# Attention weights in two sets of buffers, up to three attention tiles under way, their value chain one turn later

## The chip, the cores and the metric

The program runs on one core of a Trainium2 chip. The metric is device time in microseconds; lower is better. TensorE (PE) does matmuls and transposes, VectorE (DVE), ScalarE (ACT) and GpSimd (POOL) do the element work, and SyncE (SP) issues the DMAs. Every engine works through its own queue in order.

## The reference, cut to what matters

One layer of a hybrid encoder runs over 2048 prompt frames and 32 sample frames (model width 1024, float32). A projection gives queries (8 heads of 64), keys and values (2 heads) and the input of a state-space scan. The attention is banded by chunks of 64 frames, with a learned sink per head:

```python
s = einsum('bnqgrd,bnkgd->bngrqk', q, k) * HEAD_DIM ** -0.5
m = maximum(max(s, axis=-1), sink)
p = exp(s - m[..., None])
p = p / (sum(p, axis=-1) + exp(sink - m))[..., None]
o = einsum('bngrqk,bnkgd->bnqgrd', p, v)
```

Each chunk sees its own 64 frames and the 128 before. Attention and scan outputs are normalised, joined and projected (`w_out`), and a gated feed-forward follows.

## The kernel before, in words

Float32 products are made of three matmuls on operands split into a high and a low part: `split` copies the high part on ScalarE and subtracts on VectorE, and `mm3` issues the three matmuls. The kernel has four stages. Stage A (to about 355 us) projects. Stage B (about 355 to 560 us) runs the 32 scan groups (tiles `v`, `y`, `w`), six deferred projections (`qp`, `kp`) and the first six attention tiles. Stage C (about 560 to 950 us) runs the other eleven attention tiles beside the scan's gate (`c_prep`, bank `cb`), the norms (`c_norm`) and the output projection (`c_out`, banks `co`). The feed-forward fills the rest.

Stages B and C interleave Python generators. `Flow(make, n, width, lag)` holds at most `width` of them, starts the next when the youngest has had `lag` turns, and gives each one turn per `step`, oldest first. A turn is what stands between two `yield`s. This gives the source order. The builder's planner then orders each engine's instructions: among those that are ready by its own estimate of time, the one earliest in source order goes first. The order is fixed when the kernel is built; on the chip an engine waits at the head of its queue.

An attention tile is 128 query frames, and its work for the two 64-frame halves is numbered o = 0 and 1. Its turns before the change: (1) load `qkv`; (2) split and transpose queries and keys (`qb`, `kb`); (3) and (4) scores (`s`) and `softmax` of half 0 and half 1 into `pbuf` 0 and 1; (5) `p_split` of half 0, first key head: transposes of the weights into `pt`, then the split into `th`, `tl`; (6) the second key head; (7) `p_values` of half 0 (`ob`) and `p_split` of half 1; (8) its second key head; (9) `p_values` of half 1; (10) the end. With width 2 and lag 5 a new tile starts every five turns at the soonest. `softmax` takes the maximum on VectorE, four exponentials and one for the sink on ScalarE, a sum and a reciprocal on VectorE, and one scaling of `pbuf` on GpSimd.

In stage C each pass of the loop gives one turn to attention, one to `c_prep`, one to `c_norm` and two (`CST`) to `c_out`, which takes about five passes per tile. An attention tile starts only when it is less than `NATT` = 6 ahead of the tiles that `c_out` has finished. `c_norm` squares the attention output (`sqa`, GpSimd), sums it (`sa`, VectorE), adds over partitions with two pairs of tiny matmuls (`rb`) and takes the power (`rso`, GpSimd); `c_out` fills two banks `co` per half of the width, and `t<-co,rso` on ScalarE and then VectorE empty them, which needs `rso`. Scores, `pt`, `ob`, `qb` and `kb` share two PSUM banks in stage B and rotate over these and the `cb` banks in stage C. `th` and `tl` have two buffers each. When all attention tiles are done, `ffn_open` opens the feed-forward's buffers.

Of the kernel before, what the change touches and what calls it, by code (L numbers as in the profile page):

```python
# [10 lines left out]
F32 = mybir.dt.float32  # L11
# [12 lines left out]
NT = NPT + 1  # L24
# [49 lines left out]
def hybrid_kernel(  # L74
# [10 lines left out]
    V, A, P, PE, SP = nc.vector, nc.scalar, nc.gpsimd, nc.tensor, nc.sync  # L85
# [17 lines left out]
    def f(a):  # L103
        return a.bitcast(F32)

    def cp(e, out, a):
        if e is A:
            act(out, a)
        else:
            e.tensor_copy(out, a)  # L110

    def split(hi, lo, src, eh, el):
        cp(eh, hi, src)
        tt(el, lo, src, f(hi), SUB)

    def mm(out, lhsT, rhs, start, stop, more=False):
        PE.matmul(out, lhsT, rhs, start=start, stop=stop, skip_group_check=more)  # L117
# [798 lines left out]
    pb_ = bin_.enter_context(tc.tile_pool(name="pb", bufs=1, reuse_waits="tile", side="right"))  # L916
# [92 lines left out]
    def bbank(shape, dt=F32, nm="ab"):  # L1009
        turn[0] += 1  # L1010
        if CBANK and turn[0] % 3:
            return CBANK[0](shape, dt, nm)
        if AS3 and not CBANK and turn[0] % 2:
            return AS3[0].tile(shape, dt, tag="ab", name=nm)
        return as2.tile(shape, dt, tag="ab", name=nm)
# [7 lines left out]
    ts(V, nsink, nsink, -1.0)  # L1023
    ts(V, nsinks, nsinks, -1.0)

    pe_ = [pb_.tile([128, 4, 256], F32, name=f"pbuf{o}") for o in range(2)]
    P.memset(pe_[0][:, :, 192:256], 0.0)
    P.memset(pe_[1][:, :, 0:64], 0.0)

    def kv_split(kf, vf, dst, n):  # L1030

        ks = pb2.tile([128, 2, 2, 2, HD], F32R, tag="ks", name="ks", bufs=1)
        hi = ks[0:n, :, 0]
        act(hi, kf.unsqueeze(2).to_broadcast([n, 2, 2, HD]))
        tt(V, ks[0:n, :, 1], kf.unsqueeze(2).to_broadcast([n, 2, 2, HD]), f(hi), SUB)
        kb = bbank([128, 4, 128], F32R, nm="kb")
        for i in range(4):
            PE.transpose(kb[:, i, 0:n], ks[0:n, i // 2, i % 2].rearrange("t a d -> t (a d)"), identr[0:n, 0:n])
        cp(A, dst, f(kb[:, :, 0:n]))
        vs = pb2.tile([128, 2, 2, 2, HD], F32R, tag="vs", name="vs", bufs=4)  # L1040
        hi = vs[0:n, :, 0]
        act(hi, vf.unsqueeze(2).to_broadcast([n, 2, 2, HD]))
        tt(P, vs[0:n, :, 1], vf.unsqueeze(2).to_broadcast([n, 2, 2, HD]), f(hi), SUB)
        return vs
# [18 lines left out]
    def p_split(pbuf, kbs, npair, kv):  # L1063

        nc_ = npair * 128
        pt = bbank([128, 2, 256], nm="pt")
        for i in range(npair):
            for kb in kbs:
                PE.transpose(pt[:, kb, i * 128:(i + 1) * 128], pbuf[:, kv * npair + i, kb * 128:kb * 128 + 128], ident)
        th = pb2.tile([128, 2, 256], F32R, tag="th", name="th")  # L1070
        tl = pb2.tile([128, 2, 256], F32R, tag="tl", name="tl")
        k0, k1 = kbs[0], kbs[-1] + 1
        split(th[:, k0:k1, 0:nc_], tl[:, k0:k1, 0:nc_], pt[:, k0:k1, 0:nc_], A, V)
        return th, tl

    def p_values(parts, vlist, kbs, npair, out):

        w = npair * 128
        ob = bbank([128, 2 * w], nm="ob")
        n = 3 * len(kbs)  # L1080
        for kv in range(2):
            th, tl = parts[kv]
            c = 0
            for kb in kbs:
                vs, kn = vlist[kb]
                vh, vl = (vs[0:kn, kv, i].rearrange("t a d -> t (a d)") for i in range(2))
                for a, b in ((vh, th), (vl, th), (vh, tl)):
                    mm(ob[:, kv * w:kv * w + w], a, b[0:kn, kb, 0:w], c == 0, c == n - 1)
                    c += 1
        obv = ob.rearrange("p (m x q) -> p m x q", m=4, x=2)  # L1090
        for x in range(2):
            cp(V if x else A, out[64 * x:64 * x + 64], obv[64 * x:64 * x + 64, :, x])
# [2 lines left out]
    atts = {}  # L1095

    def attention_tile(j):
        j = TILES[j]
        n = 128 if j < NPT else DEC
        qkv = pb2.tile([128, QKV], F32, tag="qkv", name="qkv", bufs=1)  # L1100
        SP.dma_start(qkv[0:n], qkv_d[j * 128:j * 128 + n])
        yield 1
        qs = pb2.tile([128, NH, 128], F32R, tag="qs", name="qs", bufs=1)
        qv = qkv[0:n, 0:512].rearrange("p (h d) -> p h d", d=HD)
        split(qs[0:n, :, 0:64], qs[0:n, :, 64:128], qv, A, P)
        qt = pb2.tile([128, NH * 128], F32R, tag="qt", name="qt", bufs=1)
        qw = n // 2 if j < NPT else n
        qtv = qt[:, 0:NH * n].rearrange("p (o h q) -> p h o q", h=NH, q=qw)
        for hb in range(2):
            qb = bbank([128, 4, 128], F32R, nm="qb")  # L1110
            for i in range(4):
                PE.transpose(qb[:, i, 0:n], qs[0:n, hb * 4 + i], identr[0:n, 0:n])
            cp(V if hb else A, qtv[:, hb * 4:hb * 4 + 4], f(qb[:, :, 0:n]).rearrange("p h (o q) -> p h o q", q=qw))
        kf = qkv[0:n, 512:640].rearrange("p (h d) -> p h d", d=HD)
        vf = qkv[0:n, 640:768].rearrange("p (h d) -> p h d", d=HD)
        kt = pb2.tile([128, 4, 256], F32R, tag="kt", name="kt")
        att = pat.tile([128, 4, 128], F32, tag="att", name="att", bufs=NATT)
        atts[j] = att
        if j < NPT:
            vcur = kv_split(kf, vf, kt[:, :, 128:256], n)  # L1120
            if j == TILES[0]:
                pkv = pb2.tile([128, 2, 128], F32, tag="ckv", name="pkv", bufs=1)
                SP.dma_start(pkv, qkv_d[(j - 1) * 128:j * 128, 512:768].rearrange("t (a d) -> t a d", a=2))
                vprev[0] = kv_split(pkv[:, 0].rearrange("p (h d) -> p h d", d=HD),
                                    pkv[:, 1].rearrange("p (h d) -> p h d", d=HD), kt[:, :, 0:128], 128)
            elif j:
                V.tensor_copy(kt[:, :, 0:128], f(vprev[1][:, :, 128:256]))
            vpt = [vprev[0], vcur]
            vprev[0], vprev[1] = vcur, kt
            yield 1  # L1130
            vlist = [(vpt[0], 128), (vcur, 128)]
            kbs = (0, 1) if j else (1,)
            for o in range(2):
                lo, hi = (64 * o, 192 + 64 * o) if j else (128, 192 + 64 * o)
                sp = [bbank([128, 2, 256], nm="s") for _ in range(2)]
                for pr in range(4):
                    for x in range(2):
                        mm(sp[pr // 2][:, pr % 2, lo:hi], qt[:, 512 * o + 128 * pr:512 * o + 128 * pr + 128],
                           kt[:, (pr // 2) * 2 + x, lo:hi], x == 0, x == 1)
                softmax(sp, pe_[o], lo, hi, nsink)  # L1140
                yield 1
            for o in range(2):
                parts = []
                for kv in range(2):
                    parts.append(p_split(pe_[o], kbs, 2, kv))
                    yield 1
                p_values(parts, vlist, kbs, 2, att[:, :, 64 * o:64 * o + 64])
        else:
            ckv = pb2.tile([128, 2, 128], F32, tag="ckv", name="ckv", bufs=1)
            SP.dma_start(ckv[:, 0], cache_k[0, 0].rearrange("t h d -> t (h d)"))  # L1150
            SP.dma_start(ckv[:, 1], cache_v[0, 0].rearrange("t h d -> t (h d)"))
            vc = kv_split(ckv[:, 0].rearrange("p (h d) -> p h d", d=HD), ckv[:, 1].rearrange("p (h d) -> p h d", d=HD),
                          kt[:, :, 0:128], 128)
            vo = kv_split(kf, vf, kt[:, :, 128:160], n)
            sp = bbank([128, 2, 256], nm="s")
            for kv in range(2):
                for x in range(2):
                    mm(sp[:, kv, 0:160], qt[:, 128 * kv:128 * kv + 128], kt[:, kv * 2 + x, 0:160], x == 0, x == 1)
            P.memset(pe_[0][:, 0:2, 160:192], 0.0)
            softmax([sp], pe_[0], 0, 160, nsinks)  # L1160
            yield 1
            parts = [p_split(pe_[0], (0, 1), 1, kv) for kv in range(2)]
            yield 1
            p_values(parts, [(vc, 128), (vo, DEC)], (0, 1), 1, att[:, :, 0:DEC])
        yield 1
# [23 lines left out]
    def stage(nm):  # L1189
        return pw1.tile([128, 512], F32, tag="tc", name=nm, bufs=TC)  # L1190

    fa = Flow(attention_tile, NT, 2, 5)
    n = 0
    while fd.next < fd.n or fd.live:
        for fl, st, lim in ((fm, FM, G), (fd, FDS, G), (fa, FAS, NATT)):
# [705 lines left out]
```

## Time and profile before

| | |
|---|---|
| median of 3 runs | 2361.86 us (2360.06 to 2366.63) |
| the profiled execution | 2357.34 us, of which its span is 2355.6 us |
| busy share of the span | PE 94%, PE weight load 87%, DVE 76%, POOL 56%, ACT 53% |
| granted TensorE clock, mean | 0.967 of full speed |

The busy share of PE is an average over stages. The change touches only the attention tiles, so the stretch to read is the one in which these run, from about 355 to 880 us. A granted clock of 1.0 is 2.4 GHz and 0.5 is 1.2 GHz; a value between is a mix of the two over the stretch. In lines of the trace L89 is the helper for two-operand element work, L101 that for ScalarE, L117 that for matmuls; L1069 is the transpose in `p_split`, L1354 the sum in `c_norm`.

### The profile page before, as it was taken

The numbers are of one execution on the slowest core, as the hardware profiler recorded it, in microseconds if no ns is written. First come the engines' busy times: TensorE is split into PE (matmuls) and PEld (weight loads), VectorE is DVE, ScalarE is ACT, GpSimd is POOL, SyncE is SP. The second block draws the span as 40 slices with busy tenths as digits, with TensorE's granted clock in tenths as the row PEclk, the third lists the DMA queues.
The fourth block names the chain that finished last, engine by engine and source line by source line (L and its number), as shares of the span: only waits on it lengthen the run. The fifth ranks groups of instructions, "written<-read, shape, count | busy, mean of one in ns | idle before, by whom it ended". The sixth has DMA issues, their size and how long they took to land. (4 is left out here: it accounts for less than half of the span.)

```text
span 2355.6 us, 39042 instructions
## 1 busy us (share of the span) xinstructions
PE 2213.2 (94%) x13286; PEld 2055.3 (87%) x13286; DVE 1784.8 (76%) x2715; ACT 1252.0 (53%) x2538; POOL 1324.1 (56%) x1193
## 2 busy tenths in 40 slices
PE   7888998998989999899999998999999989999998
PEld 4576776787788878899999998999999989999998
DVE  6978876777777774766768889666678897777887
ACT  5655534556556555544445575444455744444663
POOL 1277775785656555578884246565522465655233
PEclk8899998998999999999999999999999999999999
DMA  7757767875312215567666545543365445433653
GB/s 232 265 169 235 204 201 221 252 229 170 92 57 77 78 42 172 159 188 225 199 182 216 168 138 168 158 128 107 97 200 171 126 141 157 135 103 120 193 159 122
DMA packets 429572, 380.12 MB, mean 161 GB/s; under 512 B 57326, under 2 KB 358986, under 8 KB 429372
## 3 DMA queue, kind: packets, MB, share of 16 engines
q1 hardware_dynamic: 429372, 377.63, 52.8%
q8 instruction: 104, 1.70, 0.3%
q14 instruction: 96, 0.79, 0.1%
HBM read 284.63 MB, written 92.91 MB: 160 GB/s over the span
## 5 line engine op out<-in xcount | busy, mean ns | idle before, releaser
L89 DVE TENSOR_TENSOR wl<-wr,wh 128x512 fp32r<-128x512 f32 (+1 forms) x708 | 721.0, 1036 | 226.6 <-ACT wh L101 223.7
L101 ACT ACTIVATE wh<-wr 128x512 fp32r<-128x512 f32 (+1 forms) x708 | 430.4, 616 | 532.4 <-PE fx L117 291.4
L117 PE MATMUL fx<-bh,wh 128*128 128x352 f32 (+1 forms) x1576 | 509.6, 323 | 8.4 <-DVE acc L98 4.7
L117 PE MATMUL fx<-bl,wh 128*128 128x352 f32 (+1 forms) x1576 | 508.8, 323 | 3.1 <-DVE bl L89 3.1
L117 PE MATMUL fx<-bh,wl 128*128 128x352 f32 (+1 forms) x1576 | 509.2, 323 | 0.0
L89 POOL TENSOR_TENSOR wr<-wr 128x512 f32<-128x512 f32 x256 | 379.7, 1493 | 199.1 <-DVE wl L89 158.8
L117 PEld LDWEIGHTS fx<-bh,wh 128*128 128x128 f32 x1576 | 299.6, 190 | 10.2 <-DVE acc L98 5.2
L117 PEld LDWEIGHTS fx<-bl,wh 128*128 128x128 f32 x1576 | 299.4, 190 | 3.9 <-DVE bl L89 3.9
L117 PEld LDWEIGHTS fx<-bh,wl 128*128 128x128 f32 x1576 | 299.2, 190 | 0.1
L117 PE MATMUL fy<-bh,wh 128*128 128x352 f32 (+1 forms) x792 | 254.5, 321 | 0.0
L117 PE MATMUL fy<-bh,wl 128*128 128x352 f32 (+1 forms) x792 | 254.2, 321 | 0.0
L117 PE MATMUL fy<-bl,wh 128*128 128x352 f32 (+1 forms) x792 | 254.0, 321 | 0.0
L89 POOL TENSOR_TENSOR c<-c 128x352 f32<-128x352 f32 (+1 forms) x96 | 138.4, 1442 | 135.1 <-ACT wh L101 100.6
L89 POOL TENSOR_TENSOR c<-c,acc 128x352 f32<-128x352 f32 (+1 forms) x72 | 84.7, 1181 | 171.8 <-ACT c L101 168.4
L89 POOL TENSOR_TENSOR q<-q,q 128x1408 f32<-128x1408 f32 (+3 forms) x23 | 84.6, 3682 | 123.6 <-DVE q L89 87.3
L89 DVE TENSOR_TENSOR bl<-q,bh 128x1408 fp32r<-128x1408 f32 (+3 forms) x85 | 149.8, 1765 | 5.1 <-ACT bh L101 5.1
L117 PEld LDWEIGHTS fy<-bh,wh 128*128 128x128 f32 x792 | 149.4, 189 | 0.0
L117 PEld LDWEIGHTS fy<-bl,wh 128*128 128x128 f32 x792 | 149.3, 189 | 0.0
L117 PEld LDWEIGHTS fy<-bh,wl 128*128 128x128 f32 x792 | 149.0, 188 | 0.1
L117 PE MATMUL fz<-bh,wl 128*128 128x352 f32 (+1 forms) x412 | 134.8, 328 | 9.1 <-DVE wl L89 9.1
L117 PE MATMUL fz<-bl,wh 128*128 128x352 f32 (+1 forms) x412 | 133.8, 325 | 3.8 <-DVE bl L89 3.8
L101 ACT ACTIVATE bh<-q 128x1408 fp32r<-128x1408 f32 (+3 forms) x85 | 108.9, 1286 | 51.4 <-DVE q L89 34.2
(388 smaller groups left out, 5225.4 us busy)
## 6 DMA issues: line engine op xcount, KB each, us to landing
wr<-in_w_gate_dram SPq DMA_DIRECT2D x132, 256.0 KB
wr<-in_w_up_dram SPq DMA_DIRECT2D x132, 256.0 KB
wr<-sd_d SPq DMA_DIRECT2D x96, 256.0 KB
wr<-in_w_down_dram SPq DMA_DIRECT2D x72, 256.0 KB
adw<-in_w_ada_dram SPq DMA_DIRECT2D x64, 256.0 KB
f_d<-c SPq DMA_DIRECT2D x88, 176.0 KB
sm<-sm_d SPq DMA_DIRECT2D x32, 448.0 KB
q<-f_d SPq DMA_DIRECT2D x16, 704.0 KB
```

Of the source, the lines that this page charges most:

```text
L89: e.tensor_tensor(out, a, b, op=op)
L101: A.activation(out, a, func, **kw)
L117: PE.matmul(out, lhsT, rhs, start=start, stop=stop, skip_group_check=more)
```

## The change

There are two sets of weight buffers, `pes`, and a tile takes the set of its index's parity; each set has its never-written columns cleared once. `Flow` may hold three attention tiles. A prompt tile has an empty turn after the second softmax, and another before `p_values` of half 1. Its turns are then: (1) load, (2) queries and keys, (3) and (4) the softmaxes, (5) empty, (6) and (7) `p_split` of half 0, (8) `p_values` of half 0 with `p_split` of half 1, (9) its second key head, (10) empty, (11) `p_values` of half 1, (12) the end. The first unit of the feed-forward in plain products, which the change's name mentions, is in the kernel before as well.

```diff
--- before.py
+++ after.py
@@ -1023,9 +1023,10 @@
     ts(V, nsink, nsink, -1.0)
     ts(V, nsinks, nsinks, -1.0)
 
-    pe_ = [pb_.tile([128, 4, 256], F32, name=f"pbuf{o}") for o in range(2)]
-    P.memset(pe_[0][:, :, 192:256], 0.0)
-    P.memset(pe_[1][:, :, 0:64], 0.0)
+    pes = [[pb_.tile([128, 4, 256], F32, name=f"pbuf{i}{o}") for o in range(2)] for i in range(2)]
+    for pe_ in pes:
+        P.memset(pe_[0][:, :, 192:256], 0.0)
+        P.memset(pe_[1][:, :, 0:64], 0.0)
 
     def kv_split(kf, vf, dst, n):
 
@@ -1095,6 +1096,7 @@
     atts = {}
 
     def attention_tile(j):
+        pe_ = pes[j % 2]
         j = TILES[j]
         n = 128 if j < NPT else DEC
         qkv = pb2.tile([128, QKV], F32, tag="qkv", name="qkv", bufs=1)
@@ -1139,10 +1141,13 @@
                            kt[:, (pr // 2) * 2 + x, lo:hi], x == 0, x == 1)
                 softmax(sp, pe_[o], lo, hi, nsink)
                 yield 1
+            yield 1
             for o in range(2):
                 parts = []
                 for kv in range(2):
                     parts.append(p_split(pe_[o], kbs, 2, kv))
+                    yield 1
+                if o:
                     yield 1
                 p_values(parts, vlist, kbs, 2, att[:, :, 64 * o:64 * o + 64])
         else:
@@ -1189,7 +1194,7 @@
     def stage(nm):
         return pw1.tile([128, 512], F32, tag="tc", name=nm, bufs=TC)
 
-    fa = Flow(attention_tile, NT, 2, 5)
+    fa = Flow(attention_tile, NT, 3, 5)
     n = 0
     while fd.next < fd.n or fd.live:
         for fl, st, lim in ((fm, FM, G), (fd, FDS, G), (fa, FAS, NATT)):
```

## Rows read from the trace of the kernel before

**Rows 1.** Windows by stage: us, busy (x count) of each engine, PEclk, DMA share, GB/s.

```profile
355.00:560.00 205.00, 178.67 (x1129) 154.62 (x1127) 145.77 (x322) 106.70 (x253) 151.51 (x274) 0.97 0.71 215
...
560.00:600.00 40.00, 30.37 (x150) 24.39 (x151) 35.23 (x54) 29.89 (x70) 12.80 (x8) 0.71 0.63 199
...
640.00:880.00 240.00, 220.44 (x1396) 197.00 (x1395) 178.47 (x302) 133.37 (x385) 141.58 (x127) 0.95 0.21 65
```

**Rows 2.** Waits of TensorE, 640 to 880 us: us in total, times, longest.

```profile
PE pt L1069 <- POOL pbuf L89: 9.6, 3, 4.9
PE pt L1069 <- DVE st L89: 4.4, 1, 4.4
```

**Rows 3.** Windows around three stalls: each stall, then the stretch behind it.

```profile
683.00:687.46 4.46, 0.02 (x1) 0.00 (x1) 4.04 (x12) 3.43 (x20) 1.76 (x3) 0.50 0.00 1
687.46:692.00 4.54, 4.54 (x26) 4.54 (x26) 1.18 (x5) 1.91 (x5) 1.74 (x2) 0.50 0.00 0
...
731.00:735.50 4.50, 0.00 (x0) 0.00 (x0) 2.43 (x10) 3.51 (x18) 2.32 (x4) 0.80 0.22 77
735.50:741.50 6.00, 5.98 (x36) 5.98 (x37) 2.88 (x6) 2.77 (x5) 2.17 (x2) 0.58 0.01 3
...
829.80:834.70 4.90, 0.04 (x2) 0.01 (x1) 3.22 (x11) 3.97 (x20) 2.85 (x4) 0.80 0.29 107
834.70:841.60 6.90, 6.90 (x45) 6.90 (x46) 3.65 (x7) 4.12 (x8) 3.75 (x4) 0.65 0.00 1
```

**Rows 4.** Timeline of TensorE at the second stall: start us, us, instruction, idle before.

```profile
730.59 0.39 PE L117 MATMUL co<-woh,ml 128*128 128x512 f32 x1
735.52 1.11 PE L1069 MATMUL pt<-cpk,pbuf 128*128 128x128 f32 x4 [4.55 <-POOL pbuf L89]
736.43 0.43 PE L117 MATMUL rb<-cols,sa 128*128 128x2 f32 x2
...
741.55 0.39 PE L117 MATMUL co<-woh,ah 128*128 128x512 f32 x1
```

**Rows 5.** Timelines of VectorE, GpSimd and ScalarE at the second stall.

```profile
731.12 1.02 DVE L1354 TENSOR_REDUCE sa<-sqa 128x128 f32<-128x512 f32 x1
...
737.56 0.70 POOL L89 TENSOR_TENSOR rso<-rso,cols 128x2 f32<-128x2 f32 x1 [0.25 <-DVE rso L98]
...
738.83 0.68 ACT L101 ACTIVATE t<-co,rso 128x512 f32<-128x512 f32 x1
...
740.38 0.74 DVE L98 SCALAR_TENSOR_TENSOR t<-co,rso,t 128x512 f32<-128x512 f32 x1
```

**Rows 6.** Timelines at the first and third stall, VectorE and TensorE.

```profile
684.22 1.02 DVE L1354 TENSOR_REDUCE sa<-sqa 128x128 f32<-128x512 f32 x1
...
693.05 0.39 PE L117 MATMUL co<-woh,ah 128*128 128x512 f32 x1
...
829.92 1.00 DVE L1354 TENSOR_REDUCE sa<-sqa 128x128 f32<-128x512 f32 x1
...
841.60 0.40 PE L117 MATMUL co<-woh,ah 128*128 128x512 f32 x1
```

**Rows 7.** Tile pbuf, 640 to 880 us: why its engines sat idle, all reasons.

```profile
  DVE st L89: 37.8, 13
  POOL pbuf L89: 25.5, 7
  DVE st L1060: 7.2, 11
  ACT t L101: 0.4, 1
```

**Rows 8.** Tile th, 640 to 880 us: one line of who waited for it.

```profile
  ACT th L101: 2.9, 1
```

**Rows 9.** Timeline of TensorE where the scan stage ends.

```profile
560.88 1.94 PE L1069 MATMUL pt<-cpk,pbuf 128*128 128x128 f32 x8 [3.45 <-ACT pbuf L101]
```

**Rows 10.** Tile pbuf, 355 to 560 us: one of its two clearing instructions.

```profile
L1027 POOL MEMSET pbuf<- x1: 316/316/316, 357.3 to 357.3; 128x256 f32 x1
```

## Prediction

> **What bounds the kernel now.** I read the busy shares first, then windows by stage, then TensorE's waits in the stages the change touches, then the timelines at its longest waits. The windows by stage show that TensorE is the engine to look at: in stage C (640 to 880 us) it is busy 220.4 of 240 us, against 178.5 for VectorE and 141.6 for GpSimd [rows 1]. Behind stage C comes the feed-forward, nearly all TensorE, so a microsecond that TensorE wins in stage C should stay won. The list of waits says what its idle time there is made of: 14.0 of the 19.6 us are four waits of `pt`, the transposes of the attention weights, for the softmax that ends on GpSimd (the wait named after VectorE's `st` is the same chain) [rows 2]. Three of the four hold nearly all of it: 4.46, 4.5 and 4.9 us [rows 3].
>
> The timeline at the second of them shows why it is more than one late input. TensorE ends `co` at 731.0, and next in its queue stands `pt`, whose `pbuf` is scaled at 735.5 [rows 4]. Right behind `pt` stands `rb`, the small sum of the norm. Its input `sa` is ready at 731.12 + 1.02 = 732.14 [rows 5], so `rb` waits 4.3 us for nothing but its place. Behind `rb` hangs a chain: the power `rso`, then ScalarE's and VectorE's `t<-co,rso`, which empty the banks that the next `co` needs. So `co` comes back only at 741.55. The first and third stall read alike: `sa` is ready at 685.24 and 830.92, `co` is back at 693.05 and 841.60 [rows 6]. In the stretches between the end of a stall and the return of `co` the granted clock is 0.50, 0.58 and 0.65, after 4.5 to 4.9 us without a matmul [rows 3]: a good part of the work there runs at 1.2 GHz.
>
> **The change part by part.** *Doubled `pbuf`.* No engine's idle time around `pbuf` is put down to a transpose of the tile before: all four reasons listed are the softmax's own steps [rows 7]. Taken alone it removes no wait and is worth nothing. It is needed by the rest: with `p_split` later, the next tile's exponentials would meet it. The added clearing instructions are two of 0.316 us on GpSimd [rows 10], 0.6 us, at the start of stage B, where GpSimd is idle 53 of 205 us [rows 1]. I take nothing; at most 0.6 us.
>
> *The empty turn ahead of `p_split`.* This is the part that counts. From the second softmax to the first `p_split` there was one turn; now there are two, and from the first softmax three. Work of a whole pass of the loop comes ahead of `pt` in source order: two turns of `c_out`, one of `c_norm`, one of `c_prep`, and the next tile's load. At the stalls this work includes `rb`. With `rb` first, it starts when `sa` ends. From `rb` to the return of `co` I take two bounds. Below: `rb` to the start of the power, 737.56 - 736.43 = 1.13, plus 0.70 power, 0.68 ScalarE and 0.74 VectorE, 3.25 us with no queueing. Above: 741.55 - 736.43 = 5.12 us, as the second stall has it [rows 4, 5].
>
> The gap from the end of `co` to its return is then, for the second stall, 732.14 - 731.0 = 1.1 plus 3.25 to 5.12, 4.4 to 6.3 us, in place of 741.55 - 731.0 = 10.55. For the third 830.92 - 829.8 = 1.1 gives 4.4 to 6.2 in place of 11.8; for the first 685.24 - 683.0 = 2.2 gives 5.5 to 7.3 in place of 10.05.
>
> The small work that stood in the old gap (`pt`, `qb`, `kb`, `ob`) has still to be done. I size it as busy time by granted clock: 5.98 x 0.58 = 3.5 us, 6.90 x 0.65 = 4.5 us and, for the first, 4.54 x 0.50 = 2.3 us plus 1.0 for the last microsecond before 693.05, 3.3 us at full clock [rows 3, 6]. Some of it fits into the new gap: at least `rb` itself, about 0.5 us, at most, I take, half of it. What a stall gives back is the old gap, less the new gap, less the small work, plus what fits:
>
> - second: 10.55 - 4.4 - 3.5 + 1.75 = 4.4 down to 10.55 - 6.3 - 3.5 + 0.5 = 1.25 us
> - third: 11.8 - 4.4 - 4.5 + 2.25 = 5.15 down to 11.8 - 6.2 - 4.5 + 0.5 = 1.6 us
> - first: 10.05 - 5.5 - 3.3 + 1.65 = 2.9 down to 10.05 - 7.3 - 3.3 + 0.5 = -0.05 us
>
> Together 12.45 to 2.8 us. I take the middle, 7.6 us, since the cover for `rb` is plain but ScalarE has the exponentials in the same microseconds. What is late next is `t<-co` on ScalarE.
>
> At the seam of stages B and C `pt` waits once for 3.45 us [rows 9]. TensorE has little else there (busy 30.4 of 40 us, clock 0.71 [rows 1]), so the later turn gains between nothing and 3.45; I take half, 1.7 us. Inside stage B TensorE and GpSimd are taken up by the scan groups, which come first in source order, and `pt` hardly waits: I take nothing, and count a reshuffled order in the range.
>
> *The empty turn ahead of the last `p_values`, and the third tile.* The last `ob` comes two turns later, in the turn in which the next tile's first `p_split` is issued, just ahead of it. `c_norm` asks for the tile more than two tiles of `c_out` later, so that delay is covered. Width 3 keeps the pace at one tile per five turns; the third tile only finishes while a new one loads. The attention ends two passes later, and `ffn_open` with it; five tiles of `c_out` are left then, which cover it. Without that cover it would cost the two passes.
>
> **The sum.** 7.6 + 1.7 = 9.3 us. The profiled execution took 2357.3 us, the median of the runs is 4.5 us above it: 2348.0 in its terms, 2352.5 us as a median, 0.4% faster. A measurement of this kernel tells about 0.3%, 7 us, from no change.
>
> **The rivals.** *All stalls go.* If the planner finds TensorE enough ready work everywhere, the three waits (13.9 us), the half clock behind them (4.54 x 0.50 + 6.0 x 0.42 + 6.9 x 0.35 = 7.2 us) and the seam's 3.45 go: 24.5 us, 2337 us [rows 3, 9]. For it: most tiles of stage C already pass without a `pt` wait. Against it: `co` cannot return before `rso`. The Trainium skill (Perfetto Trace Analysis, Optimization Strategy) says that a gap which repeats on the engine that should be saturated can mean too little SBUF or PSUM for the next tile. Read as SBUF, that would make the doubled `pbuf` the cure and point to this case; the trace does not bear it out, since no idle time is put down to a buffer of `pbuf` in use [rows 7].
>
> *No change.* The stall is one of banks: the scores hold four of the shared PSUM banks until the exponentials have read them, the next tile's `qb` and `kb` come behind `pt` in the rotation, and `co` has its two. Then TensorE has nothing to run in the gap whatever the order, `rb` saves what the later `pt` costs, and the time stays at 2362, within some 5 us. For it: `qb` and `kb` do run only after `pt`. Against it: `rb` needs only one bank. Read as PSUM, the skill's rule speaks for this one; the change adds no bank, and no row here separates the two.
>
> *Slower.* `th` and `tl` have two buffers. The next tile's first split into `th` now follows the last `ob` of the tile before within one turn; before, a turn lay between them. If ScalarE reaches `th` before `ob` has read the old one, it stands still, and with it the exponentials and `t<-co` queued behind. The trace has one such wait of 2.9 us [rows 8]. Hidden behind `co` it costs nothing; at five of the ten prompt tiles in stage C, with nothing gained at the stalls, it makes 14.5 us, 2376 us. It decides from the fourth tile on (3 x 2.9 = 8.7 against 9.3 gained).
>
> **How the numbers follow.** Forecast (3 to 16 us faster): 0.50. All stalls go: 0.12. No change: 0.20. Slower: 0.18. Of the forecast's 0.50 some 0.36 lies beyond 7 us, so faster 0.48, same 0.34, slower 0.18. The forecast's own range is 2346 to 2359. With the no-change case, nearly all of the first rival and the nearer part of the slower one it is 2338 to 2371.
>
> **What would show it.** Right: `pt` waits of TensorE in stage C fall from 14 us to under 5; `rb` stands ahead of `pt` in TensorE's order; after the stalls the granted clock stays near 1.0 and the mean in stage C rises from 0.95; the feed-forward starts about 9 us earlier and lasts as long. Wrong: TensorE waits as long for `t<-co` or a bank at the same places; ScalarE's wait of `th` for `ob` grows; stage C gains and the start of the feed-forward does not; or stage B, which I left alone, becomes longer under the new order.

## The result and the profile after

The changed kernel takes 2348.12 us (median of four runs, 2346.64 to 2350.46), the kernel before 2362.66 beside it: a ratio of 0.9933 [0.9919, 0.9946], 14.5 us or 0.67% faster, where 9.3 us were forecast. The profiled execution is the one of 2346.64 us (span 2344.8); that of before, 2357.3, lies 5 us under its own median, so the two traces differ by only 10.8 us of span.

First the windows by stage of after, over the stretches of [rows 1] (us, busy and count of PE, PEld, DVE, ACT and POOL, PEclk, DMA share, GB/s):

```profile
355.00:560.00 205.00, 178.68 (x1080) 155.02 (x1079) 135.91 (x301) 103.14 (x238) 141.11 (x249) 0.92 0.69 213
560.00:600.00 40.00, 28.40 (x138) 23.11 (x137) 31.90 (x57) 29.98 (x61) 15.96 (x29) 0.74 0.67 205
640.00:880.00 240.00, 237.25 (x1519) 209.90 (x1519) 185.89 (x334) 144.62 (x419) 158.69 (x145) 1.00 0.23 74
```

In stage C TensorE's idle time falls from 19.6 to 2.8 us, and in the same 240 us 1519 matmuls stand instead of 1396. But in stage B it runs fewer, 1080 for 1129. So I cut both traces where the work cuts them: at `gsp`, the transpose with which the scan stage closes (called the last scan matmul below), at the first `rb` and at the first `fx` of the feed-forward. The line of `gsp`, before and after (its first and last start stand at the end):

```profile
L1229 PE MATMUL gsp<-cpk,gsm x1: 332/332/332, 555.8 to 555.8; 128*128 128x128 f32 x1
```

```profile
L1234 PE MATMUL gsp<-cpk,gsm x1: 327/327/327, 583.5 to 583.5; 128*128 128x128 f32 x1
```

Windows from the first `rb` to the first `fx`, "stage C" from here on, before and then after:

```profile
600.30:955.40 355.10, 330.35 (x2013) 289.15 (x2012) 245.15 (x408) 196.22 (x519) 206.86 (x190) 0.96 0.29 90
```

```profile
618.10:946.10 328.00, 321.81 (x2014) 280.62 (x2013) 233.53 (x404) 193.19 (x516) 203.45 (x190) 1.00 0.31 95
```

The work is the same (2013 and 2014 matmuls) and takes 27.1 us less: 18.6 us of idle time (24.8 to 6.2) and 8.5 us of busy time, with the granted clock up from 0.96 to 1.00. Against this, stage C begins 17.8 us later, and the feed-forward is 1.5 us shorter: 17.8 - 27.1 - 1.5 = -10.8, the whole difference of the spans. A gain of more than three times the forecast's 7.6 and a loss that it didn't have made a number close to it.

The list of TensorE's waits in the stretch of [rows 2], after:

```profile
PE co L117 <- ACT t L101: 1.1, 2, 0.7
PE pt L1070 <- POOL pbuf L89: 0.7, 2, 0.4
PE ob L117 <- ACT th L101: 0.4, 1, 0.4
PE s L117 <- DVE att L110: 0.3, 1, 0.3
```

The waits of `pt` fall from 14.0 us to 0.7. To see where they went, take one tile from the scores of half 0 to the moment when its weights are scaled. Before, at the second stall, on TensorE and GpSimd:

```profile
722.14 1.03 PE L117 MATMUL s<-kt,qt 128*128 128x192 f32 x8
...
734.00 1.47 POOL L89 TENSOR_TENSOR pbuf<-pbuf,st 128x768 f32<-128x768 f32 x1 [0.73 <-DVE st L1060]
```

The timelines of after in the middle of stage C, TensorE, GpSimd and ScalarE, to be held against these and [rows 4, 5]:

```profile
725.33 1.12 PE L117 MATMUL s<-kt,qt 128*128 128x192 f32 x8
...
729.44 1.12 PE L117 MATMUL s<-kt,qt 128*128 128x192 f32 x8
...
735.72 0.28 PE L117 MATMUL rb<-cols,sa 128*128 128x2 f32 x2
...
740.25 1.04 PE L1070 MATMUL pt<-cpk,pbuf 128*128 128x128 f32 x8
...
743.36 0.50 PE L117 MATMUL co<-woh,ah 128*128 128x512 f32 x1 [0.66 <-ACT t L101]
```

```profile
737.77 1.47 POOL L89 TENSOR_TENSOR pbuf<-pbuf,st 128x768 f32<-128x768 f32 x1
```

```profile
732.07 0.66 ACT L101 ACTIVATE t<-co,rso 128x512 f32<-128x512 f32 x1
732.64 0.40 ACT L101 ACTIVATE pbuf<-s,st 128x192 f32<-128x192 f32 x1
```

The chain is no shorter than it was: from the scores to the scaled `pbuf` it takes 13.3 us before (722.14 to 735.47) and 13.9 after (725.33 to 739.24). But now TensorE has `co`, `ob` and `rb` to run until `pbuf` is there, and the lines of after wait 0.66 us at most. The return of `co` after `rb` is no quicker either: 743.36 - 735.72 = 7.6 us, more than the prediction's upper bound of 5.12, with `pt` and other work in between. What fills the time is `co` work into a bank that ScalarE emptied at 732.07, ahead of the exponentials.

What begins later is stage B. Its load of the first attention tile, on SyncE's queue, before and after:

```profile
355.57 0.43 SPq L1101 DMA_DIRECT2D qkv<-qkv_d  x1
```

```profile
369.36 0.58 SPq L1103 DMA_DIRECT2D qkv<-qkv_d  x1
```

The change adds no work ahead of this load but two clearings, yet it comes 13.8 us later. In the program as built, `qkv` lies in other memory: before, in the place of small tiles of scan parameters; after, 8 KB further, in the place of operands of the projection stage that ends there (`hl` among them). On SyncE's queue its load now stands behind eleven loads of the scan, issued from 360.62 us on. Whether that matters, and not the order of turns, is what the experiments had to tell apart.

### The profile page after: what moved, and what is told of

Read it like the earlier page. It is cut to its first block, busy times and chain, and to the rows that moved or that the text cites. A ratio compares the mean times of both kernels' runs of the same rounds, so it can differ in the third digit from the quotient of the medians.

```text
span 2344.8 us, 39041 instructions
## 1 busy us (share of the span) xinstructions
PE 2215.2 (94%) x13286; PEld 2055.6 (88%) x13286; DVE 1770.5 (76%) x2715; ACT 1258.6 (54%) x2544; POOL 1326.1 (57%) x1195
## 5 line engine op out<-in xcount | busy, mean ns | idle before, releaser
L101 ACT ACTIVATE wh<-wr 128x512 fp32r<-128x512 f32 (+1 forms) x708 | 430.3, 616 | 529.7 <-PE fx L117 290.7
L101 ACT ACTIVATE bh<-q 128x1408 fp32r<-128x1408 f32 (+3 forms) x85 | 108.9, 1286 | 52.5 <-DVE q L89 35.1
```

The lines of the kernel that those rows point to most:

```text
L101: A.activation(out, a, func, **kw)
```

## The experiments

Each ratio is against the kernel before in runs on the same chip. Positions are from each kernel's trace, in us. "One set" and "two sets" count the sets of `pbuf`; "place" says whether the tiles behind them lie where they did before.

| kernel | ratio | median | first load | last scan matmul | first `rb` | stage C | `pt` waits in C |
|---|---|---|---|---|---|---|---|
| before | 1 | 2363.0 | 355.6 | 555.8 | 600.3 | 355.1 | 14.5 |
| before_again | 1.0004 [0.9990, 1.0018] | 2365.1 | 356.7 | 559.0 | 603.8 | 361.4 | 14.4 |
| after | 0.9933 [0.9919, 0.9946] | 2348.1 | 369.4 | 583.5 | 618.1 | 328.0 | 0.7 |
| turns_c_only: two sets, turns from the seventh tile | 0.9947 [0.9930, 0.9965] | 2352.5 | 373.1 | 570.9 | 608.6 | 344.3 | 5.4 |
| turns_b_only: two sets, turns in the first six tiles | 1.0004 [0.9991, 1.0017] | 2363.8 | 368.3 | 584.0 | 619.2 | 346.0 | 6.5 |
| pbuf_only: two sets, no turns, width 2 | 0.9920 [0.9898, 0.9942] | 2346.6 | 371.3 | 563.4 | 600.7 | 347.0 | 8.7 |
| pad_only: before, place moved | 0.9921 [0.9904, 0.9938] | 2345.4 | 371.3 | 564.6 | 601.2 | 349.6 | 8.7 |
| one_pbuf: one set, all turns, old place | 0.9891 [0.9868, 0.9915] | 2339.8 | 359.1 | 556.2 | 605.4 | 330.6 | 0.7 |
| one_pbuf_pad: one set, all turns, place moved | 0.9929 [0.9914, 0.9945] | 2348.2 | 371.5 | 583.9 | 617.9 | 329.1 | 1.0 |
| one_first: one set, only the first empty turn | 0.9920 [0.9902, 0.9939] | 2344.7 | 357.9 | 556.4 | 606.9 | 338.6 | 0.9 |
| one_last: one set, only the last empty turn | 0.9997 [0.9984, 1.0010] | 2363.8 | 356.7 | 562.3 | 613.2 | 353.2 | 12.9 |
| one_width2: one set, all turns, width 2 | 0.9952 [0.9935, 0.9970] | 2350.5 | 356.0 | 555.0 | 601.2 | 340.6 | 0.5 |
| one_c_only: one set, turns from the seventh tile | 0.9882 [0.9867, 0.9898] | 2336.6 | 358.1 | 558.6 | 603.0 | 330.5 | 0.7 |
| early_rb: before, `rb` one turn earlier | 1.0054 [1.0036, 1.0073] | 2375.9 | 356.1 | 563.3 | 607.6 | 367.4 | 14.3 |

**turns_c_only and turns_b_only.** The empty turns only in the tiles of stage C, or only in those of stage B. The theory: the turns of stage C gain, those of stage B lose. The edit on after (`<` in place of `>=` for the second):

```diff
         pe_ = pes[j % 2]
+        wait = j >= NATT
         j = TILES[j]
...
-            yield 1
+            if wait:
+                yield 1
...
-                if o:
+                if o and wait:
                     yield 1
```

> The empty turns only for the tiles that start in stage C (index 6 and up); the first six tiles keep the old turns. In the profile of the changed kernel the stretch from the first rb to the first matmul of the feed-forward is 27 us shorter (355.1 to 328.0) and the start of that stretch is 18 us later (600.3 to 618.1). Theory: both come from the empty turns, the gain from those of stage C and the loss from those of stage B. Then this kernel keeps the 27 us and loses nothing: about 2336 us, with the last y matmul back near 551 us. Rival: the loss in stage B comes from the doubled buffers or from a planner order that any edit redraws; then the scan stage ends late here too and the time stays near 2348 us.

> The empty turns only for the first six tiles. Theory: stage B loses what it lost, up to 18 us, and stage C keeps its stalls of pt (14 us of waits, as before the change): 2370 to 2381 us. Rival: the loss of stage B is not due to the turns, or is made up at the seam: about 2362 us.

Measured: 2352.5 and 2363.8 us. The stage B turns alone bring the whole delay of the last scan matmul (584.0) and leave the total where it was. But turns_c_only is not better than after: its last scan matmul comes earlier (570.9), and its stage C is 16 us longer. Both still have the late first load, with no turn to blame for it in turns_c_only. Up to the last scan matmul turns_c_only has the same order on every engine as pad_only below (564.6), so its 570.9 says nothing of turns.

**pbuf_only.** The two sets alone, by the edit above with `wait = False`, and:

```diff
-    fa = Flow(attention_tile, NT, 3, 5)
+    fa = Flow(attention_tile, NT, 2, 5)
```

> Two sets of weight buffers, but width 2 and no empty turns. Theory: no engine waited for a buffer of weights in use, so nothing changes: 2362 us within 4 us, and the three waits of pt in stage C are there as before. Rival: repeated gaps mean too few buffers; then the gain of the change is here: about 2348 us.

Measured: 0.9920. The part that I had costed at nothing gives, alone, as much as the whole change. Its first load comes at 371.3.

**pad_only, one_pbuf and one_pbuf_pad** separate the second set as a buffer from the 8 KB that it takes. One_pbuf is after with `for i in range(1)` and `pe_ = pes[0]`. The pad is memory that nothing reads, added to before and to one_pbuf:

```diff
+    pad = [pb_.tile([128, 4, 256], F32, name=f"pad{o}") for o in range(2)]
+    P.memset(pad[0][:, :, 192:256], 0.0)
+    P.memset(pad[1][:, :, 0:64], 0.0)
```

> The changed kernel with a single set of weight buffers. Theory: with the value chain later, the next tile's exponentials now meet weights that are still to be transposed, ScalarE waits for pt in stage C, and part of the gain goes: 2352 to 2362 us. Rival: the exponentials come after the transposes anyway, and the second set has no part in the gain: 2348 us within 4 us.

> The kernel before with 8 KB per partition more in the pool of the weight buffers, cleared like a second set and then never used. Doubled buffers alone were as fast as the whole change, and in every kernel with two sets the first load of qkv was issued 12 to 18 us later than with one set. Theory A, place: the second set acts by its place only, it pushes the tiles behind it to other addresses and so changes the planner's order; then this kernel does what doubled buffers alone did: about 2347 us, first qkv load near 370 us. Theory B, use: the second set is worth something because exponentials no longer follow the transposes of the tile before; then this one is as before: about 2363 us, whatever the first load does.

> The changed kernel with a single set and the same 8 KB left unused. Place: as the changed kernel, about 2348 us, with the first qkv load near 370 us and the scan stage ending near 583 us. Use: as the kernel with a single set, about 2340 us.

Measured: pad_only equals pbuf_only (0.9921 and 0.9920) and one_pbuf_pad equals after (0.9929 and 0.9933); each pair has the same order of instructions on every engine, buffer numbers aside. One_pbuf is faster than after (0.9891; the two intervals end 0.0004 apart). So the second set does nothing as a buffer, under the old turns or the new. Its size moves the tiles behind it. The first load shows it, in pad_only and then in one_pbuf:

```profile
371.25 0.58 SPq L1104 DMA_DIRECT2D qkv<-qkv_d  x1
```

```profile
359.12 0.43 SPq L1103 DMA_DIRECT2D qkv<-qkv_d  x1
```

Under the old turns that move is worth some 17 us; under the new ones it costs some 8 (2339.8 to 2348.2), at the edge of what these runs can tell: the intervals of one_pbuf and one_pbuf_pad touch. Read the other way: at the old place the turns and the third tile give 23 us, at the new place nothing (2345.4 to 2348.2, intervals that overlap).

**one_first, one_last and one_width2** take one_pbuf apart: without the turn ahead of the last `p_values`, without the turn ahead of `p_split`, and with width 2.

```diff
# one_first
-                if o:
-                    yield 1
# one_last
                 yield 1
-            yield 1
             for o in range(2):
# one_width2
-    fa = Flow(attention_tile, NT, 3, 5)
+    fa = Flow(attention_tile, NT, 2, 5)
```

> A single set, and only the empty turn ahead of p_split. By the prediction's reasoning this turn alone takes the waits of pt in stage C away: about 2340 us, like the single set with both turns, and less than 3 us of pt waits between the first rb and the feed-forward. Rival: the order is redrawn by every edit, and which stalls remain is chance; then the time lies anywhere from 2340 to 2363 us with stalls of pt of 5 us and more.

> A single set, and only the empty turn ahead of the last p_values. The turn ahead of p_split alone took the waits of pt away (0.9 us) and left stage C at 338.6 us, both turns 330.6. Theory: the last p_values has no part in the waits of pt, so the stalls of 4 to 5 us are back and the time is near 2363 us; at most the 8 us between 338.6 and 330.6 are kept, 2355 us. Rival: any shift of source order does it, and this one is near 2345 us too.

> A single set and both empty turns, but two tiles under way at most. A tile lives 12 turns, so two tiles take 12 turns and not 10, while c_out takes five passes per tile. Theory: the attention falls behind in source order by one turn per tile; in stage C it has a lead of some tiles, so 2340 us as with three tiles, or a few us more. Rival: the third tile is needed for the pace, stage C waits for attention, 2350 us and more.

Measured: one_first 2344.7, one_last 2363.8, one_width2 2350.5. TensorE's waits of `pt` in stage C, in one_last and then in one_first, where other waits stand above them:

```profile
PE pt L1070 <- POOL pbuf L89: 12.9, 5, 3.7
```

```profile
PE co L117 <- DVE t L98: 5.9, 4, 2.9
PE co L117 <- ACT t L101: 2.8, 3, 1.8
...
PE pt L1070 <- POOL pbuf L89: 0.9, 1, 0.9
```

With three tiles and at the old place, the turn ahead of `p_split` takes the waits of `pt` away by itself, and the last turn alone does nothing. Together they are 5 us under the first alone, but the intervals overlap, so that stays open. Beside both turns the third tile is worth 10.7 us (0.9891 against 0.9952). In the trace of one_width2 stage C is 10.0 us longer than in one_pbuf but begins 4.2 earlier, and the feed-forward is 9.2 us longer (1397.8 against 1388.6); why it should be was not followed up. With width 2 and the longer tiles a new tile comes every six turns instead of five, so this kernel changes the pace as well.

**early_rb.** The prediction put the gain down to `rb` standing ahead of `pt`. This kernel ends `c_norm` one turn sooner, in before: `rb` and the power move up, the next norm starts sooner, and the planner's order changes from there on:

```diff
-QY = 2
+QY = 1
```

> The kernel before, attention untouched, with one turn less between the sum of c_norm and rb (QY 1 for 2), so that rb is issued one turn sooner. In the changed kernel rb stands ahead of pt at every tile of stage C and the waits of pt are 0.7 us for 14.5. If rb's place is what the stalls hang on, rb goes ahead of pt here too, the long stalls fall to some 2.5 us each, and stage C shrinks by about 8 us: 2355 us. If the later softmax wait is what counts, whatever rb does, pt still waits about 14 us and the time stays at 2363 us.

Measured: 1.0054, 13 us slower. `rb` does stand ahead of `pt` at the stall of [rows 4]. Its timelines there, TensorE, ScalarE, VectorE and GpSimd:

```profile
738.40 0.28 PE L117 MATMUL rb<-cols,sa 128*128 128x2 f32 x2
...
739.32 0.40 PE L117 MATMUL co<-woh,ml 128*128 128x512 f32 x1
745.24 0.79 PE L117 MATMUL co<-woh,ah 128*128 128x512 f32 x1 [5.52 <-ACT t L101]
...
749.93 1.04 PE L1069 MATMUL pt<-cpk,pbuf 128*128 128x128 f32 x8
```

```profile
741.05 0.42 ACT L101 ACTIVATE pbuf<-s,st 128x192 f32<-128x192 f32 x1 [2.53 <-DVE st L89]
...
744.40 0.21 ACT L101 ACTIVATE st<-st 128x4 f32<-128x4 f32 x1
744.49 0.69 ACT L101 ACTIVATE t<-co,rso 128x512 f32<-128x512 f32 x1
```

```profile
742.78 0.16 DVE L98 SCALAR_TENSOR_TENSOR rso<-rb,cols 128x2 f32<-128x2 f32 x1
```

```profile
743.01 0.70 POOL L89 TENSOR_TENSOR rso<-rso,cols 128x2 f32<-128x2 f32 x1 [1.02 <-DVE st L89]
```

TensorE now waits 5.52 us for `t<-co`. Most of it is VectorE's order: it comes to `rso<-rb` at 742.78, 4 us after `rb`, behind maxima, a gate and the next `sa`. The power ends at 743.71, and the exponentials ahead of `t<-co` on ScalarE then cost at most 0.8 us more. The gap, from the end of `co` (739.72) to its return, is 5.5 us, inside the prediction's bounds of 4.4 to 6.3. But `pt` still waits, even where `rb` stands 7 us ahead of it, as at the longest stall of this kernel:

```profile
843.95 0.30 PE L117 MATMUL rb<-cols,sa 128*128 128x2 f32 x2
...
851.25 1.97 PE L1069 MATMUL pt<-cpk,pbuf 128*128 128x128 f32 x8 [6.77 <-POOL pbuf L89]
```

The list of waits of this kernel in 600 to 955 us shows that `pt` waits as long as before, with new waits beside it:

```profile
PE pt L1069 <- POOL pbuf L89: 14.3, 3, 6.8
PE co L117 <- ACT t L101: 7.7, 2, 5.5
PE rb L117 <- ACT pbuf L101: 3.6, 1, 3.6
```

**one_c_only.** The edits of turns_c_only on one_pbuf: one set at the old place, three tiles, turns only from the seventh tile on.

> A single set, and the empty turns only for the tiles that start in stage C. Stage B is then issued exactly as before the change, so the first rb should be at 600 us as before. If the turns of stage C carry the gain, stage C takes about 330 us and the whole about 2338 us. If a redrawn order is all there is, stage C takes 340 to 355 us: 2348 to 2363 us.

Measured: 2336.6 us, 0.9882 [0.9867, 0.9898], 11.5 us under the change, the best of the study. Its stage C, against the two windows shown for before and after:

```profile
603.00:933.50 330.50, 321.21 (x2008) 280.11 (x2007) 241.64 (x408) 193.76 (x517) 205.42 (x190) 1.00 0.31 96
```

It has after's stage C (330.5 us, clock 1.00) and nearly before's start of it (603.0). Against one_pbuf (2339.8) the intervals overlap. Against turns_c_only, which has the same turns at the moved place, it is 16 us faster (0.9882 and 0.9947, intervals apart), with 0.7 us of `pt` waits for 5.4: so the place also decides what the turns of stage C are worth.

**before_again** is before without an edit, to see how far two traces of one program differ.

> The kernel before, unchanged, profiled a second time: its median is that of before, and the stretch from the first rb to the feed-forward and the stalls of pt show how far two executions of one program differ. 355 us and 14.5 us of pt waits, within 3 us, if stages read from one trace may be compared as they stand.

Measured: 1.0004 [0.9990, 1.0018]. Its stage C:

```profile
603.80:965.20 361.40, 336.25 (x2013) 294.10 (x2012) 245.75 (x408) 196.69 (x519) 207.14 (x190) 0.95 0.29 89
```

That is 6.3 us longer than in the other trace of the same program, while the `pt` waits agree (14.4 and 14.5). Four kernels (before, before_again, early_rb, one_c_only) have the same order on every engine up to the last scan matmul, and it stands at 555.8, 559.0, 563.3 and 558.6. So a position or a stage from one trace is good to some 7 us. The 27 us of stage C and the 28 us of the last scan matmul are well beyond that, the 8 us of the last scan matmul in pbuf_only and pad_only lie at its edge, and differences like 328.0 against 330.6 are not beyond it.

## Why the prediction was right, and where it was not

**The time.** 2348.1 us lies 4.4 under the forecast and inside its own range. The feed-forward starts 9.3 us earlier in the trace (955.4 to 946.1), as the sum said, and lasts as long (1388.6 and 1387.1). But before_again's feed-forward starts at 965.2, so the 9.3 us hold against one trace only. And the agreement is luck, a sum of two errors: a stage C that gained 27.1 instead of 7.6 and a stage B side that lost 17.8 instead of gaining 1.7.

**"With `rb` first", the middle of 4.4 to 6.3 us.** This is the step that failed in stage C. `pt` waits fell from 14 to 0.7 us, `rb` stands ahead of `pt` in the stretch shown, and the clock stays at 1.00, all as foretold. But the new gap is not the chain from `sa` to `co`: there is no gap. The forecast moved `rb` into the old order and left the other engines' order as it was; early_rb comes nearest to that case, though its order changed elsewhere too, and it is slower, with 14.3 us of `pt` waits. So `rb` ahead of `pt` is not enough. What the empty turn does, by the timelines of after, is put other `co` work between the scores and `pt`, into banks emptied in time. The rival "all stalls go" described this, and its price of 24.5 us was close; that against it, "`co` cannot return before `rso`", holds only if `rso` belongs to the `co` that fills the gap. That the turn ahead of `p_split` does it is shown, at the old place and with three tiles, by one_first and one_last. Which engine's new order matters most was not tried: early_rb's rows point to VectorE, after's to ScalarE.

**"Taken alone it removes no wait and is worth nothing."** Of the four reasons that the prediction called the softmax's own steps, the last (`ACT t L101`, 0.4 us) is not one; none is a transpose, so the reading holds. The sentence is right for the second set as a buffer: with or without it, at the same place, the times are equal (0.9929 and 0.9933, 0.9921 and 0.9920). It is wrong for the effect, since its 8 KB move other tiles, which is worth 17 us under the old turns. And "it is needed by the rest" is wrong: one_pbuf does without and is not slower than after, but 8 us faster. The Trainium skill (Perfetto Trace Analysis, Optimization Strategy) says that a gap which repeats on the engine to be saturated can mean too little SBUF or PSUM for the next tile. For these gaps the runs decide against it: a second set of buffers brought no more than an equal amount of memory that nothing reads, and the gaps went without either. No kernel of the study had more PSUM banks.

**"Inside stage B I take nothing, and count a reshuffled order in the range."** The 27.7 us by which the last scan matmul came later (555.8 to 583.5) are here. Neither part does it alone: it comes at 563 to 571 with the moved place and the old turns in stage B (pbuf_only, pad_only, turns_c_only), at 556.2 with the turns at the old place; place and stage B turns together end at 583.5, 584.0 and 583.9. Some of it comes back at the seam (44.5 us from the last scan matmul to the first `rb` before, 34.6 after), where 1.7 us had been forecast. That the prediction named a longer stage B among the signs against it did not make it a term of the sum.

**The third tile**, "keeps the pace at one tile per five turns", was costed at nothing in its own right. It is worth 10.7 us beside the turns, partly in stage C and partly in the feed-forward; the turns without it still give 0.9952.

**The other rivals.** No change through banks: TensorE did find work in the gap, with no bank added, so that is out. Slower through `th`: the wait of ScalarE for `th` shows up once in 640 to 880 us, at 1.4 us, against 2.9 before [rows 8]:

```profile
  ACT th L101: 1.4, 1
```

**What stays open.** Why the moved place helps the old turns and hurts the new ones. Under the old turns it shows in stage C, where the `pt` waits fall from 14.5 to 8.7 us and the feed-forward starts at 947.7 and 950.8 against 955.4 and 965.2 in the two traces of before. Under the new ones it shows in stage B (first `rb` at 617.9 against 605.4) and, where only stage C has the turns, in stage C too (344.3 against 330.5). The pad kernels show that the move of 8 KB is the cause; that it works through the late first load, and not through another tile that moved with it, was not tried, nor was putting the second set elsewhere. The order of the fastest kernels (2336.6, 2339.8) is not settled either.

## What to carry to other kernels

When a queue waits for a long chain over other engines, put more source order between the chain's start and its consumer, with one more tile in flight to cover it, and look at the order of every engine in the chain: moving the victim behind the wait (`rb`) ahead of it left the wait as long and added others. Before you credit added buffers, time them against the same memory unused; here the memory's place was worth 17 us one way and 8 the other, and the buffers nothing. Try such a delay in the stage whose trace shows the wait, and without the change of memory: in stage C alone, at the old place, it gave 2336.6 us, 27 under before and 11.5 under the change. But the same turns at the moved place gave 2352.5, and in all stages at the old place they gave 2339.8, which the runs don't tell from 2336.6.

## What the runs showed of the hardware

The busy time of the same 2013 or 2014 matmuls fell from 330.35 to 321.81 us when the stalls went, with the granted clock up from 0.96 to 1.00: a third of stage C's gain between these two traces, 8.5 of 27.1 us, was clock and not idle time. The busy part varies from trace to trace and the idle part hardly does: before_again has 336.25 us busy at a clock of 0.95, 5.9 more than before, and 25.2 us idle against 24.8. The kernels without the `pt` waits (after, one_c_only) have 321.2 to 321.8 us busy, at 1.00.
